# A hybrid RWKV-7 / FoX block on one core: product stages of several streams joined in bursts, FoX beside the RWKV chain, the lane inversion on GpSimd

## The chip, the core and the metric

The kernel runs on one core of a Trainium2 chip. A core has five engines with their own instruction queues: TensorE (matrix products and transposes, PE in the profile), VectorE (DVE), ScalarE (ACT), GpSimd (POOL) and SyncE (SP, which here only issues transfers). Each queue is worked off in its order, and an instruction may wait on semaphores of the others. The metric is the device time of one execution in microseconds.

## The reference, cut to what matters

One decoder block over 272 tokens (16 meta tokens and 256 of the input), width 2048. Two mixers run side by side, each with 16 heads of 64, and their outputs are gated and added; a SwiGLU feed-forward part follows.

```
proj = rms(h) @ w_in                          # RWKV, FoX and gate columns
y_a  = rwkv7(...)                             # below
y_b  = fox(...)                               # softmax attention with a forget gate
merged = sig(z_ga) * (y_a @ w_a) + sig(z_gb) * (y_b @ w_b)
h = h + merged @ w_o
h = h + (silu(gate) * up) @ w_down            # gate, up = rms(h) @ w_gu

def step(S, inp):                             # RWKV-7, a scan over the tokens, per head
    r_t, w_t, k_t, v_t, a_t, b_t = inp
    sa = einsum('bhvk,bhk->bhv', S, a_t)
    S  = S * w_t[:, :, None, :] + sa[..., None] * b_t[:, :, None, :] \
       + v_t[..., None] * k_t[:, :, None, :]
    return S, einsum('bhvk,bhk->bhv', S, r_t)
```

## The kernel before, in words

**Weight stream.** All weights come from memory in blocks of 128 x 1024 FP32 (`wload`). The SP queue loads a block into one of three `raw` tiles; ScalarE rounds it into `wh` (L322), VectorE forms the rest `wl = raw - wh` (L323), and TensorE multiplies both parts (L333 to L335, L392 and L394). Three tiles each of `raw`, `wh` and `wl` set how far the loads run ahead. A block of the projection holds 256 columns by 512 rows, so each of `k`, `v`, `r` and each gate needs four blocks.

**Order of the weight stream.** For each of four groups of four heads: `rwkv_jobs` (k, v, r, then the small decay and gate products), `fox_jobs` (q, k, v) and, after the first three groups, two gate tiles `zg` (four blocks each). The remaining gates follow group 3. `run` emits the load of a block ahead of the products of the block before it.

**Streams beside it.** Everything that isn't weight stream is written as generators ("streams"): `rwkv_bg` (the RWKV chain of a group), `fox_bg` (the attention of a group), `sums` and `norms` (FoX norms). A stream runs one stage up to its next `yield`, and the yielded number is the distance to its next stage in estimated ns of TensorE time. After every few weight products `slot` (L361) looks which streams are due and emits one stage of the one that has been due longest; `GAP` and `MIX` then keep the next one away. So the distances and `slot` fix at which place among the weight products a stage's products stand on TensorE, whose order is kept as it is written. On the other queues the framework places the instructions; what they hold is read from their order.

**RWKV chain.** In chunks of 64 tokens: `mat` products give the matrices NK; their strictly triangular 32 x 32 blocks go through memory (`d1`, L765 to L773) into `ln`, one matrix a lane, 112 lanes. Then the lane inversion (L831 to L838): 31 steps of two operations on `lx`, with growing rows, 62 dependent VectorE operations. The result goes from `lx` to memory (`d2`, `d3`, L841 and L843) and back into `X` (L847, L848), all issued on SP. After the distance `LANE` the stages `rhs`, `QT`, `X` follow, and then for each of four chunks `rhs`, `u` with `y`, `s` with `y`. The transposes `trbk`, `trv`, `tr0` prepare operands ahead of the inversion.

**FoX.** Per group and half (m = 0, 1): a bias on GpSimd (L1064 to L1070), scores `sc`, softmax, transposes `ppt` and `ptm`, and the product `po` with the values. The second half started after the first had ended.

PSUM has eight banks; four belong to the weight stream (`PSM`), four to the streams.

Of the kernel before, what the change touches and what calls it, by code (L numbers as in the profile page):

```python
# [62 lines left out]
LANE = 24000  # L63
GAP = 250
LERP = 2800
BIAS = 7000
STEP = 1000
NORM = 4200
SUMS = 2000
X_RS = 1400  # L70
X_SPREAD = 1400
X_V = 1900
X_SC = 1600
X_EXP = 1100
X_DIV = 2600
X_PT = 1400
Y_SQ = 1400
# [6 lines left out]
Y_BONUS = 1200  # L84
Y_TRBK = 1400
Y_TRV = 1100
Y_TR0 = 1600
Y_RHS = 1400
Y_U = 1400
Y_XT = 1400  # L90
Y_QT = 1200
Y_GN = 1400
# [5 lines left out]
def hybrid_block(ctx, tc, A, out, dbg=None):  # L98
# [18 lines left out]
    def aux_ps(name):  # L117
        return psa.tile([P, 512], F32, tag="aux", name=name)
# [224 lines left out]

    def spawn(gen, delay):
        streams.append([clock[0] + delay, gen])

    def stage(st):
        try:
            st[0] = clock[0] + (next(st[1]) or HOP)
        except StopIteration:  # L350
            streams.remove(st)

    def pe_mm(out_, lhsT, rhs, start, stop, skip=False):
# [316 lines left out]
    def rwkv_bg(g, box):  # L670
# [15 lines left out]
        nc.scalar.activation(sq, kk, AF.Square)  # L686
        yield Y_SQ
        kn_ = rw.tile([P, 12], F32, tag="kn", name=f"kn{g}", bufs=2)
# [4 lines left out]
        backs = [spread(kr_, m, L, f"kx{g}{m}") for m in range(2)]  # L693
        yield Y_SPREAD
        for m in range(2):
# [37 lines left out]
        split(*parts, sq[:, :, :T])  # L733
        yield Y_AB

# [3 lines left out]
        for m in range(2):  # L739
            pss = [aux_ps(f"mat{g}{m}{h}") for h in range(2)]  # L740
            for c in range(4):
                for h in range(2):
                    pe_mm(pss[h][:, c * P:(c + 1) * P], bk[hb(h), m, c].rearrange("p x t -> p (x t)"),
                                     ar[hb(h), :, m, tok(c)], start=True, stop=True)
            for h in range(2):
                nc.vector.tensor_tensor(NK[:, h, 4 * m:4 * m + 4, :], pss[h].rearrange("p (c w) -> p c w", w=P),
                                        bcast(mup, 4), op=ALU.mult)
            yield Y_MAT
        pss = [aux_ps(f"mat0{g}{h}") for h in range(2)]
# [28 lines left out]
        for h in range(2):  # L778
            for m in range(2):
                nc.gpsimd.tensor_copy(NK[0:HD, h, 4 * m:4 * m + 4, 0:HD],  # L780
                                      ar[hb(h), 0, m, NMETA:].rearrange("p (c t) -> p c t", t=HD))
        yield Y_NEXT

        bo = ot(f"bo{g}")
        for m in range(2):
# [5 lines left out]
            nc.gpsimd.tensor_scalar(bo[:, m, :], bo[:, m, :], vi("gn_b", m), None, op0=ALU.add)  # L791
        yield Y_BONUS

# [5 lines left out]
        for m in range(2):  # L799
            ps = aux_ps(f"trbk{g}{m}")  # L800
            for c in range(4):
                pe_tr(ps[:, c * P:(c + 1) * P], bkf[:, 4 * m + c, :], ident)
            nc.scalar.activation(BK[:, :, 4 * m:4 * m + 4, :].rearrange("p h c d -> p c h d"),
                                 ps.rearrange("p (c h d) -> p c h d", h=2, d=HD), AF.Copy)
            yield Y_TRBK
        ps = aux_ps(f"trv{g}")
# [7 lines left out]
        yield Y_TRV  # L814
        ps = aux_ps(f"tr0{g}")
# [15 lines left out]
        for s_ in range(31):  # L831
            n, w = s_ // 3 + 1, 31 - s_
            tv, xv = lt[:, 0:n, s_ + 1:], lx[:, 0:n, s_ + 1:]
            nc.vector.tensor_tensor(tv, lx[:, 0:n, s_:s_ + 1].to_broadcast([LANES, n, w]),
                                ln[:, s_:s_ + 1, s_ + 1:].to_broadcast([LANES, n, w]), op=ALU.mult)
            nc.vector.tensor_tensor(xv, xv, tv, op=ALU.add)
            if s_ % 4 == 3:
                yield STEP  # L838
# [10 lines left out]
        yield LANE  # L849

# [3 lines left out]
        def step(c, S, BK, SV, NK, X, Y):  # L854
# [24 lines left out]
            for h in range(2):  # L879
                nc.vector.tensor_copy(SV[0:nt, h, mine, :], pv2(ps)[h * HD:h * HD + nt])  # L880
            yield Y_U
            if not last:
# [20 lines left out]
            if not first:  # L903
                nc.scalar.activation(Y.rearrange("p (m c) v -> p m c v", m=2)[:, :, c, :], pv2(psy), AF.Copy)
            yield HOP

# [7 lines left out]
        next(meta_steps)  # L914
        yield Y_XT
        ps = aux_ps(f"QT{g}")
# [6 lines left out]
        next(meta_steps)  # L923
        yield Y_QT
        ps = aux_ps(f"X12{g}")
# [22 lines left out]
        nc.vector.tensor_tensor(Y, Y, s2.unsqueeze(2).to_broadcast([P, 8, HD]), op=ALU.mult)  # L948
        yield NORM
        ps = aux_ps(f"yT{g}")  # L950
# [28 lines left out]
    def fox_jobs(g):  # L979
# [18 lines left out]
        def norms():  # L998
            while len(done) < 2:
                yield  # L1000
            yield from rsqrt_steps(fx, hr, hs, [P, 20], "ht")
            yield X_RS

            nc.vector.tensor_tensor(hs[:, 0:8], hs[:, 0:8], hr[:, 0:8], op=ALU.mult)
            backs = [spread(hr[:, 8:20], m, L, f"fx{g}{m}") for m in range(2)]
            yield X_SPREAD
            for m in range(2):
                nc.vector.tensor_tensor(kn[:, m, :], kn[:, m, :], backs[m](), op=ALU.mult)
            yield
            ready.append(1)  # L1010

        def post(dst, n):
            def f(pss):
# [14 lines left out]
                if dst is vv:  # L1028
                    spawn(fox_bg(g, qn, kn, vv, hs, hr, ready), HOP)
                else:  # L1030
                    spawn(sums(sqs, dst, n), SUMS)
                    if dst is kn:
                        spawn(norms(), PREP)
# [5 lines left out]
    def fox_bg(g, qn, kn, vv, hs, hr, ready):  # L1039
# [18 lines left out]
        cmb = cmask.unsqueeze(1).to_broadcast([P, 2, P])  # L1058
        for m in range(2):

# [13 lines left out]
            nq = [NMETA + P, L]  # L1074
            cq_ = [slice(0, nq[0]), slice(nq[0], nq[0] + nq[1])]
# [5 lines left out]
            for t in range(2):  # L1081
                n = nq[t]
                for h in range(2):
                    s = sc_t[h, t]
                    nm = fx.tile([P, 1], F32, tag="nm", name=f"nm{g}{m}{h}{t}", bufs=4)
                    bb = b1[:, h, :] if t == 0 else bias[:, h, :]
                    nc.vector.tensor_tensor_reduce(s[:, :n], pss[h][:, cq_[t]], bb, 1.0, -3.0e38, op0=ALU.add,
                                                   op1=ALU.max, accum_out=nm)
                    r = hr[:, qc(t, m, h)]
                    nc.vector.tensor_scalar(nm, nm, -1.0, r, op0=ALU.mult, op1=ALU.mult)  # L1090
                    nc.scalar.activation(s[:, :n], s[:, :n], AF.Exp, scale=r, bias=nm,
                                         accum_out=sums[:, 2 * t + h:2 * t + h + 1])
            yield X_SC + X_EXP
# [5 lines left out]
            yield X_DIV  # L1099


            ptm = aux_ps(f"ptm{g}{m}")
            pts = []
            for h in range(2):
                ppt = aux_ps(f"ppt{g}{m}{h}")
                for c, t, k in ((T - 96, 0, 1), (0, 0, 0), (P, 1, 0), (T + 32, 1, 1)):
                    pe_tr(ppt[:, c:c + P], sc_t[h, t][:, k * P:(k + 1) * P], ident)
                pe_tr(ptm[:NMETA, h * P:(h + 1) * P], sc_t[h, 1][:, 2 * P:L], ident)
                pT = fx.tile([P, 416], F32, tag="pT", name=f"pT{g}{m}{h}", bufs=2)
                nc.scalar.activation(pT, ppt[:, :416], AF.Copy)  # L1110
                pts.append(pT)
            nc.scalar.activation(pM[:NMETA], ptm[:NMETA, :2 * P].rearrange("p (h q) -> p h q", h=2)[:, :, 96:], AF.Copy)
            yield X_PT
            po = aux_ps(f"po{g}{m}")
            for i in range(3):
                for h in range(2):
# [9 lines left out]
            yield  # L1126

# [263 lines left out]
```

## Time and profile before

| | |
|---|---|
| Median of three timed runs | 1566.58 us (1565.39 to 1569.84) |
| The profiled execution | 1564.75 us, of which the span of its instructions 1563.0 us |
| TensorE | 10,225 instructions |
| VectorE | 1,854 instructions, the inversion 248 of them |
| GpSimd | 194 instructions |
| Granted TensorE clock | 1.000 |
| Bytes moved | 283.33 MB, 181 GB/s on average |

The profile is of one execution. Busy time is the union of an engine's instructions; times in the timeline run from the span's start. The streams end at about 607 us, with the last transposes `yT`; what follows (the rest of the gates, branch products, output projection, feed-forward part) the change doesn't touch.

### The profile page before, as it was taken

The page shows a single profiled execution, that of the slowest core. Times are in us where ns is not written, and L with a number is a line of the kernel's source. Part 1 is how long each engine was busy: PE and PEld are TensorE (multiplying, and loading weights), DVE is VectorE, ACT ScalarE, POOL GpSimd, SP SyncE. Part 2 cuts the span into 40 slices and gives each one's busy share as a digit, 9 for nine tenths or more (in the row PEclk, how much of TensorE's full clock was granted, in tenths as well). Part 3 has the DMA queues.
Part 4 walks back from the last instruction along what each step waited for, and adds up shares of the span by engine and source line. Part 5 has one row for each costly group of instructions (what it writes and reads, how often), then busy time and mean ns, then how long its engine had stood idle before and what let it go on. Part 6 is the DMA issues. An engine that isn't in the chain of part 4 may idle for free.

```text
span 1563.0 us, 26173 instructions
## 1 busy us (share of the span) xinstructions
PE 1553.5 (99%) x10225; PEld 1366.3 (87%) x10225; DVE 1015.7 (65%) x1854; ACT 766.8 (49%) x1118; POOL 104.3 (7%) x194
## 2 busy tenths in 40 slices
PE   9999999999999999999999999999999999999998
PEld 9999988989889888999888888888888888888887
DVE  7878688677768856875655666566566656444443
ACT  6655455465445544654445554454445544333332
POOL 2121103102203100000000000000000000000000
PEclk9999999999999999999999999999999999999999
DMA  7556546546545566777666666666666666666664
GB/s 243 173 154 173 158 126 179 157 119 168 166 135 148 161 182 192 248 225 227 189 182 179 188 186 190 188 188 189 188 189 189 185 193 187 188 202 199 187 200 131
DMA packets 211483, 283.33 MB, mean 181 GB/s; under 512 B 23888, under 2 KB 128352, under 8 KB 211360
## 3 DMA queue, kind: packets, MB, share of 16 engines
q1 hardware_dynamic: 206752, 277.53, 60.8%
q10 hardware_dynamic: 4608, 4.13, 0.8%
q8 instruction: 80, 1.31, 0.4%
q14 instruction: 43, 0.35, 0.1%
HBM read 274.43 MB, written 7.19 MB: 180 GB/s over the span
## 4 chain that ended last, share of the span: by engine, by line
PE 94%; DVE 3%; DMA 1%; ACT 1%; issue 1%; SPq 0%; POOL 0%; DVEq 0%; ACTq 0%
PE up L392 10%; PE gt L392 10%; PE zg L392 7%; PE dn L1255 5%; PE dn L1253 5%; PE dn L1254 5%; PE up L394 5%; PE gt L394 5%; PE zg L394 3%; PE f L333 2%; PE f L392 2%; PE f L335 2%; PE f L334 2%; PE br L334 2%; PE br L335 2%; PE br L333 2%
## 5 line engine op out<-in xcount | busy, mean ns | idle before, releaser
L323 DVE TENSOR_TENSOR wl<-raw,wh 128x1024 fp32r<-128x1024 f32 (+1 forms) x496 | 605.3, 1221 | 439.7 <-ACT wh L322 437.8
L322 ACT ACTIVATE wh<-raw 128x1024 fp32r<-128x1024 f32 (+1 forms) x496 | 521.2, 1052 | 624.5 <-PE dn L1254 144.4
L392 PE MATMUL gt<-hts,wh 128*128 128x512 f32 x704 | 245.0, 394 | 0.0
L392 PE MATMUL up<-hts,wh 128*128 128x512 f32 x704 | 244.9, 394 | 0.0
L394 PE MATMUL gt<-hts,wl 128*128 128x256 f32 x660 | 186.2, 282 | 0.0
L394 PE MATMUL up<-hts,wl 128*128 128x256 f32 x660 | 186.0, 282 | 0.0
L392 PE MATMUL zg<-xhl,wh 128*128 128x512 f32 x512 | 184.3, 403 | 0.0
L392 PEld LDWEIGHTS up<-hts,wh 128*128 128x128 f32 x704 | 130.1, 188 | 26.4
L392 PEld LDWEIGHTS gt<-hts,wh 128*128 128x128 f32 x704 | 130.1, 188 | 26.3
L1254 PE MATMUL dn<-wh,acl 128*128 128x512 f32 x352 | 139.5, 396 | 0.0
L1253 PE MATMUL dn<-wh,ach 128*128 128x512 f32 x352 | 139.5, 396 | 0.0
L1255 PE MATMUL dn<-wl,ach 128*128 128x512 f32 x352 | 139.5, 396 | 0.0
L394 PE MATMUL zg<-xhl,wl 128*128 128x256 f32 x480 | 135.0, 281 | 0.0
L394 PEld LDWEIGHTS up<-hts,wl 128*128 128x128 f32 x660 | 124.7, 189 | 1.8
L394 PEld LDWEIGHTS gt<-hts,wl 128*128 128x128 f32 x660 | 124.7, 189 | 1.8
L392 PEld LDWEIGHTS zg<-xhl,wh 128*128 128x128 f32 x512 | 94.5, 188 | 20.8 <-issue 1.8
L394 PEld LDWEIGHTS zg<-xhl,wl 128*128 128x128 f32 x480 | 90.6, 189 | 1.1
L1255 PEld LDWEIGHTS dn<-wl,ach 128*128 128x128 f32 x352 | 66.3, 188 | 16.2
L1254 PEld LDWEIGHTS dn<-wh,acl 128*128 128x128 f32 x352 | 66.3, 188 | 16.2
L1253 PEld LDWEIGHTS dn<-wh,ach 128*128 128x128 f32 x352 | 66.3, 188 | 16.1
L333 PE MATMUL f<-xhl,wh 128*128 128x272 f32 x256 | 77.7, 303 | 0.0
L335 PE MATMUL f<-xhl,wl 128*128 128x272 f32 x256 | 73.8, 288 | 0.0
(459 smaller groups left out, 2777.6 us busy)
## 6 DMA issues: line engine op xcount, KB each, us to landing
raw<-in_w_gate_up_dram SPq DMA_DIRECT2D x176, 512.0 KB, 3.6
raw<-in_w_in_dram SPq DMA_DIRECT2D x160, 512.0 KB, 4.2
raw<-in_w_down_dram SPq DMA_DIRECT2D x88, 512.0 KB, 4.7
raw<-in_w_o_dram SPq DMA_DIRECT2D x32, 512.0 KB, 4.6
raw<-in_w_branch_a_dram SPq DMA_DIRECT2D x16, 512.0 KB, 3.9
raw<-in_w_branch_b_dram SPq DMA_DIRECT2D x16, 512.0 KB, 3.8
zgd<-zg ACTq DMA_DIRECT2D x30, 128.0 KB, 2.4
gate<-zgd SPq DMA_DIRECT2D x15, 256.0 KB, 5.8
```

Of the source, the lines that this page charges most:

```text
L322: nc.scalar.activation(wh[:prow, cs_], raw[:prow, cs_], AF.Copy)
L323: nc.vector.tensor_tensor(wl[:prow, cs_], raw[:prow, cs_], wh[:prow, cs_].bitcast(F32), op=ALU.subtract)
L333: nc.tensor.matmul(ps, wh, ah, start=first, stop=False)
L334: nc.tensor.matmul(ps, wh, al, start=False, stop=False)
L335: nc.tensor.matmul(ps, wl, ah, start=False, stop=last)
L392: nc.tensor.matmul(ps.rearrange("p (a t) -> p a t", a=2), wh, act, start=first, stop=last)
L394: nc.tensor.matmul(ps[:, :T], wl, act[:, 0, :], start=False, stop=False)
L1253: nc.tensor.matmul(box[t], ah[:, kt, ts_], wh[:, k, :], start=first, stop=False)
L1254: nc.tensor.matmul(box[t], al[:, kt, ts_], wh[:, k, :], start=False, stop=False)
L1255: nc.tensor.matmul(box[t], ah[:, kt, ts_], wl[:, k, :], start=False, stop=last)
```

## The change

It has four parts.

1. **Bursts.** A yield may now give a second number, the PSUM banks that the stage after it needs; a stage with such a number is a product stage. `slot` emits a due stage without products first and alone, as before. Otherwise it takes all due product stages, in the order in which they came due, as long as their banks together are at most four, and emits them one behind the other. If there is only one, it holds it back by up to `HOLD` = 2000 when another that would fit is due within that time.
2. **Distances.** Several are longer, among them `X_SPREAD`, `X_PT`, `Y_TRBK`, `Y_QT`; `BIAS` goes from 7000 to 28000. Three yields are dropped, so that the transposes of bk, and those of v with tr0, are one stage each.
3. **FoX.** The bias of the second half is emitted during the first half, its scores in the stage of the first half's `po`. The small transposes into the bank `ptm` go into a free part of `ppt`, with one copy for each head into pM in place of one for both.
4. **Inversion.** The 62 operations run on GpSimd in place of VectorE. Each waits for the one before it, as on VectorE.

```diff
-    def spawn(gen, delay):
-        streams.append([clock[0] + delay, gen])
+    def spawn(gen, delay, banks=0):
+        streams.append([clock[0] + delay, gen, banks])
...
-        due = [st for st in streams if st[0] <= clock[0]]
-        if due:
+        due = sorted((st for st in streams if st[0] <= clock[0]), key=lambda st: st[0])
+        group = [st for st in due if not st[2]][:1]
+        if due and not group:
+            banks = 0
+            for st in due:
+                if banks + st[2] <= 8 - PSM:
+                    group.append(st)
+                    banks += st[2]
+            if (len(group) == 1 and clock[0] < due[0][0] + HOLD and
+                    any(st[2] and st[0] > clock[0] and st[0] < due[0][0] + HOLD and banks + st[2] <= 8 - PSM
+                        for st in streams)):
+                return
+        if group:
             clock[2] = 0.0
-            stage(min(due, key=lambda st: st[0]))
+            for st in group:
+                stage(st)
             clock[1] = clock[0] + max(GAP, MIX * clock[2])
...
-            yield Y_RHS
+            yield Y_RHS, 2
...
             tv, xv = lt[:, 0:n, s_ + 1:], lx[:, 0:n, s_ + 1:]
-            nc.vector.tensor_tensor(tv, lx[:, 0:n, s_:s_ + 1].to_broadcast([LANES, n, w]),
-                                ln[:, s_:s_ + 1, s_ + 1:].to_broadcast([LANES, n, w]), op=ALU.mult)
-            nc.vector.tensor_tensor(xv, xv, tv, op=ALU.add)
+            nc.gpsimd.tensor_tensor(tv, lx[:, 0:n, s_:s_ + 1].to_broadcast([LANES, n, w]),
+                                    ln[:, s_:s_ + 1, s_ + 1:].to_broadcast([LANES, n, w]), op=ALU.mult)
+            nc.gpsimd.tensor_tensor(xv, xv, tv, op=ALU.add)
             if s_ % 4 == 3:
                 yield STEP
...
-        for m in range(2):
+        def biases(m):
...
-            yield BIAS
+            return b1, bias
...
+        bs = biases(0)
+        yield BIAS, 2
+        sums = scores(0, *bs)
+        for m in range(2):
             yield X_SC + X_EXP
...
+            if m == 0:
+                bs = biases(1)
+            yield X_DIV, 2
-            ptm = aux_ps(f"ptm{g}{m}")
             pts = []
             for h in range(2):
                 ppt = aux_ps(f"ppt{g}{m}{h}")
+                pe_tr(ppt[:NMETA, 3 * P:], sc_t[h, 1][:, 2 * P:L], ident)
...
-                pe_tr(ptm[:NMETA, h * P:(h + 1) * P], sc_t[h, 1][:, 2 * P:L], ident)
                 pT = fx.tile([P, 416], F32, tag="pT", name=f"pT{g}{m}{h}", bufs=2)
                 nc.scalar.activation(pT, ppt[:, :416], AF.Copy)
+                nc.scalar.activation(pM[:NMETA, h, :], ppt[:NMETA, 480:], AF.Copy)
                 pts.append(pT)
...
+            if m == 0:
+                sums = scores(1, *bs)
             nc.scalar.activation(yb[:, 2 * g + m, :], po[:, :T], AF.Copy)
```

What this does to the queues shows at two places. The first is the SP queue from the last transfers of group 0's matrices into `ln` to the transfers of its inverse into `X` (`raw` are weight blocks, `d` the blocks in memory). Before:

```order
L773 DMA ln_1477<-d_1474 4x1024 x4
L318 DMA raw<-in_w_in_dram 128x4x256 x7
L1064 DMA bias_2016<-ncd 128x544
L318 DMA raw<-in_w_in_dram 128x4x256 x4
L841 DMA d_1475<-lx_1666 352x1x32 x2
L841 DMA d_1475<-lx_1666 32x10x32
L843 DMA d_1476<-lx_1666 16x1x32 x4
L847 DMA X_1668<-d_1475 32x8x32 x3
```

In the changed kernel (a line number of before is 2 to 18 higher here):

```order
L791 DMA ln_1512<-d_1509 4x1024 x4
L320 DMA raw<-in_w_in_dram 128x4x256 x6
L858 DMA d_1510<-lx_1699 352x1x32 x2
L858 DMA d_1510<-lx_1699 32x10x32
L860 DMA d_1511<-lx_1699 16x1x32 x4
L864 DMA X_1701<-d_1510 32x8x32 x3
```

The transfers that wait for `lx` stand five weight blocks earlier, behind six blocks after `ln` in place of eleven. The first block behind them is the third block of group 1's `k`; before it was the fourth of its `v`. In the other groups they move by six, five and six blocks.

The second is TensorE at group 0's first chunk, among the products of the next group's `r`. Before, the stages u and y stand apart from everything else, and so does each FoX stage:

```order
L335 MATMUL r_1_2366<-xhl,wl 128x258
L355 MATMUL u_2425<-R_2406,X_1668 64x64 x4
L355 MATMUL y_2430<-S0-1_2342,ar_1275 64x64 x4
L333 MATMUL r_1_2366<-xhl,wh 128x258
```

In the changed kernel the transposes of the second half's probabilities follow in the same burst:

```order
L337 MATMUL r_1_2250<-xhl,wl 128x258
L360 MATMUL u_2463<-R_2410,X_1701 64x64 x4
L360 MATMUL y_2468<-S0-1_2325,ar_1284 64x64 x4
L364 MATMUL ppt_2475<-ident,s_165 16x128
L364 MATMUL ppt_2475<-ident,s_164 128x128 x2
L364 MATMUL ppt_2475<-ident,s_165 128x128 x2
L364 MATMUL ppt_2484<-ident,s_167 16x128
L364 MATMUL ppt_2484<-ident,s_166 128x128 x2
L364 MATMUL ppt_2484<-ident,s_167 128x128 x2
L335 MATMUL r_1_2250<-xhl,wh 128x258
```

FoX's second half now runs through the RWKV chain in such bursts. In the whole program the bursts between weight products go from 157 to 103, with the same number of products.

More of the change, by code (lines that the diff above doesn't have):

```diff
@@ L64 @@
 GAP = 250
+HOLD = 2000
 LERP = 2800
-BIAS = 7000
+BIAS = 28000
 STEP = 1000
@@ L70 @@
 X_RS = 1400
-X_SPREAD = 1400
+X_SPREAD = 2400
 X_V = 1900
@@ L75 @@
 X_DIV = 2600
-X_PT = 1400
+X_PT = 2200
+X_PT0 = 4400
 Y_SQ = 1400
@@ L84 @@
 Y_BONUS = 1200
-Y_TRBK = 1400
-Y_TRV = 1100
+Y_TRBK = 2600
 Y_TR0 = 1600
[L88 to L91, printed above, removed]
+Y_RHS = 1600
+Y_U = 1600
+Y_XT = 1600
+Y_QT = 2200
 Y_GN = 1400
@@ L342, in hybrid_block @@
     clock = [0.0, 0.0, 0.0]
-    def spawn(gen, delay):
-        streams.append([clock[0] + delay, gen])
+    def spawn(gen, delay, banks=0):
+        streams.append([clock[0] + delay, gen, banks])
     def stage(st):
         try:
-            st[0] = clock[0] + (next(st[1]) or HOP)
+            step = next(st[1]) or HOP
         except StopIteration:
             streams.remove(st)
+            return
+        step, st[2] = step if isinstance(step, tuple) else (step, 0)
+        st[0] = clock[0] + step
     def pe_mm(out_, lhsT, rhs, start, stop, skip=False):
@@ L686, in rwkv_bg @@
         nc.scalar.activation(sq, kk, AF.Square)
-        yield Y_SQ
+        yield Y_SQ, 1
         kn_ = rw.tile([P, 12], F32, tag="kn", name=f"kn{g}", bufs=2)
@@ L693, in rwkv_bg @@
         backs = [spread(kr_, m, L, f"kx{g}{m}") for m in range(2)]
-        yield Y_SPREAD
+        yield Y_SPREAD, 2
         for m in range(2):
@@ L733, in rwkv_bg @@
         split(*parts, sq[:, :, :T])
-        yield Y_AB
+        yield Y_AB, 2
         NK = nkt(f"NK{g}")
@@ L880, in step @@
                 nc.vector.tensor_copy(SV[0:nt, h, mine, :], pv2(ps)[h * HD:h * HD + nt])
-            yield Y_U
+            yield Y_U, 2
             if not last:
@@ L904, in step @@
                 nc.scalar.activation(Y.rearrange("p (m c) v -> p m c v", m=2)[:, :, c, :], pv2(psy), AF.Copy)
-            yield HOP
+            yield (HOP, 0) if last else (HOP, 1)
         S = [None]
@@ L914, in rwkv_bg @@
         next(meta_steps)
-        yield Y_XT
+        yield Y_XT, 2
         ps = aux_ps(f"QT{g}")
@@ L923, in rwkv_bg @@
         next(meta_steps)
-        yield Y_QT
+        yield Y_QT, 2
         ps = aux_ps(f"X12{g}")
@@ L1028, in f @@
                 if dst is vv:
-                    spawn(fox_bg(g, qn, kn, vv, hs, hr, ready), HOP)
+                    spawn(fox_bg(g, qn, kn, vv, hs, hr, ready), HOP, 2)
                 else:
-                    spawn(sums(sqs, dst, n), SUMS)
+                    spawn(sums(sqs, dst, n), SUMS, 1)
                     if dst is kn:
@@ L1092, in fox_bg @@
                                          accum_out=sums[:, 2 * t + h:2 * t + h + 1])
+            return sums
+        bs = biases(0)
+        yield BIAS, 2
+        sums = scores(0, *bs)
+        for m in range(2):
             yield X_SC + X_EXP
```

24 lines of the change are left out of this document (11 added, 13 removed).

## The prediction

> **What bounds the kernel now.** I read the page's table of busy time first, then the list of waits on TensorE, and then the timeline of single stretches.
>
> ```profile
> span 1563.0 us, 26173 instructions
> PE 1553.5 (99%) x10225; PEld 1366.3 (87%) x10225; DVE 1015.7 (65%) x1854; ACT 766.8 (49%) x1118; POOL 104.3 (7%) x194
> ...
> PE po L355 <- ACT pT L1110: 1.7, 1, 1.7
> PE warmup L296 <- DVE yb L293: 1.1, 1, 1.1
> ```
>
> TensorE has work for 99% of the span, and its longest wait in the whole run is 1.7 us. So the time is the length of TensorE's list of instructions, and an edit pays in two ways only: by a shorter list, or by a wait that the list did not have. All sums below stand against the profiled execution: 1564.75 us, of which 1563.0 are span and 1.75 lie around it. The median of the timed runs, 1566.58, is 0.1% above it. A difference of about 0.3% (4.7 us) is what a measurement of this kernel can tell from none.
>
> **What joining saves.** Three places of TensorE's timeline (start, duration, engine, line, result and operands): a lone stage of FP32 products, two such stages in one burst, and a stage of transposes, each among the weight-stream products of a projection.
>
> ```profile
> 178.21 0.28 PE L335 MATMUL r<-xhl,wl 128*128 128x258 f32 x1
> 178.42 0.45 PE L355 MATMUL rhs<-sv,NK 128*64 128x64 f32 x8
> 178.80 0.39 PE L333 MATMUL r<-xhl,wh 128*128 128x258 f32 x1
> 179.03 0.28 PE L334 MATMUL r<-xhl,wh 128*128 128x258 f32 x1
> ...
> 180.60 0.28 PE L335 MATMUL r<-xhl,wl 128*128 128x258 f32 x1
> 180.81 0.45 PE L355 MATMUL u<-R,X 64*64 64x64 f32 x8
> 181.09 0.40 PE L355 MATMUL y<-S0-1_2342,ar 64*64 64x64 f32 x8
> 181.42 0.39 PE L333 MATMUL r<-xhl,wh 128*128 128x258 f32 x1
> 181.64 0.28 PE L334 MATMUL r<-xhl,wh 128*128 128x258 f32 x1
> ...
> 113.64 0.29 PE L335 MATMUL f<-xhl,wl 128*128 128x272 f32 x1
> 113.77 0.60 PE L359 MATMUL trbk<-ident,bk 128*128 128x128 f32 x4
> 114.12 0.37 PE L333 MATMUL f<-xhl,wh 128*128 128x272 f32 x1
> 114.33 0.29 PE L334 MATMUL f<-xhl,wh 128*128 128x272 f32 x1
> ```
>
> Each r product starts 0.12 us after the one before when nothing lies between. From the last one before a burst to the second one behind it, two such steps, 0.24 us, are the stream's own. The lone stage takes 179.03 - 178.21 - 0.24 = 0.58 us for 8 products. Stages u and y together take 181.64 - 180.60 - 0.24 = 0.80 us for 16. Two lone ones would take 1.16, so a join of two such stages saves about 0.35 us: the entry and the exit. Four transposes take 114.33 - 113.64 - 0.25 = 0.44 us, 0.11 each, with no such fixed part; I price their joins at nothing.
>
> In the order of before, 100 stretches of FP32 products stand alone in the weight stream. In the changed order there are 75, of which some 70 border the stream and the rest border transposes. So 25 to 30 entries go: 25 x 0.35 = 9 us saved, 11 at most (30), and 7 if a change between FP32 products and transposes costs most of a fixed part too. The number of products is the same, 8,996 rows in both orders. Beside it the 1.7 us wait of stage po may go.
>
> **What the longer distances cost.** Weight products fill them, so nothing, as long as results are not wanted: the last stage, yT of head group 3, moves by 18 weight products and still has 124 of them ahead of the branch projections. The two narrower copies into pM (8 more on ACT, which is 49% busy) hide too. The freed VectorE time is worth nothing, since TensorE waits for VectorE nowhere for more than 1.1 us.
>
> **What the inversion on GpSimd costs.** The 62 operations of a group become one chain on GpSimd, and who waits for its end is the SP queue. In that queue's order, the seven transfers of lx into d2 and d3 wait for lx, and then six transfers into X follow. Behind them stand the weight loads. Before, at head group 0:
>
> ```profile
> 121.52 0.27 PE L359 MATMUL tr<-ident,v 128*16 128x128 f32 x1
> ...
> 121.74 0.31 POOL L716 MEMSET bk<- 128x256 f32 x1 [4.46 <-PE tr L359]
> ...
> 139.60 12.23 SPq L318 DMA_DIRECT2D raw<-in_w_in_dram  x4
> 153.37 1.98 SPq L841 DMA_DIRECT2D d<-lx  x3
> ...
> 161.06 1.52 SPq L318 DMA_DIRECT2D raw<-in_w_in_dram  x3
> ...
> 153.16 0.18 DVE L836 TENSOR_TENSOR lx<-lx,lt 112x11 f32<-112x11 f32 x1
> ...
> 165.19 1.06 ACT L322 ACTIVATE wh<-raw 128x1024 fp32r<-128x1024 f32 x1 [3.20 <-DMA raw<-in_w_in_dram]
> ...
> 166.28 1.23 DVE L323 TENSOR_TENSOR wl<-raw,wh 128x1024 fp32r<-128x1024 f32 x1 [3.00 <-ACT wh L322]
> ```
>
> The last operation on lx ends at 153.34, SP issues the first transfer 0.03 us later, and the next weight block is issued only at 161.06, three at once, since their buffers had been free. That block is split at 166.28 + 1.23 = 167.51. So a block queued behind the inversion is ready **14.2 us after the inversion's end**. Before this did no harm: eleven weight loads stood between ln and d, the held block was the fourth of v, and TensorE's list of waits has none on a split of it.
>
> The change leaves only six there. The held block in group 0 is the third of k, and between it and the tr transposes TensorE has 90 gate products and 48 products of k, with no burst among them:
>
> ```profile
> 120.49 0.39 PE L392 MATMUL zg<-xhl,wh 128*128 128x512 f32 x1
> ...
> 120.84 0.40 PE L392 MATMUL zg<-xhl,wh 128*128 128x512 f32 x1
> ...
> 144.12 0.29 PE L333 MATMUL k<-xhl,wh 128*128 128x272 f32 x1
> 144.25 0.29 PE L334 MATMUL k<-xhl,wh 128*128 128x272 f32 x1
> ```
>
> A pair of gate products takes 0.35 us and a k product 0.13: 45 x 0.35 + 48 x 0.13 = 22.0 us. In the other groups, counted the same way, it is 60 pairs, 24 k products and 1.1 us of transposes, 25.2; 50 pairs and 48 k products, 23.7; and 70 pairs with 0.7 us of transposes, 25.2. The chain starts about 0.5 us after the last tr transpose, since the reset of bk, which waits for tr, stands ahead of it on GpSimd (121.74 + 0.31 against 121.52). If the chain takes D, TensorE waits D + 14.2 + 0.5 less that time: D - 7.3, D - 10.5, D - 9.0 and D - 10.5. The sum over four groups is **4D - 37.3**.
>
> Now D. Nothing in the trace shows this operation on GpSimd; the nearest rows are these.
>
> ```profile
> L445 POOL TENSOR_TENSOR zd<-z x24: 612/640/1611, 52.3 to 445.7; 128x272 f32<-128x272 f32 x16, 128x256 f32<-128x256 f32 x8
> ...
> L1069 POOL TENSOR_TENSOR b<-b,cmask x8: 722/736/1702, 110.5 to 527.6; 128x256 f32<-128x256 f32 x8
> ...
> L138 POOL TENSOR_SCALAR_AFFINE_SELECT mup<-mup x4: 233/236/240, 2.3 to 2.9; 64x64 f32<-64x64 f32 x4
> ...
> L780 POOL COPY NK<-ar x16: 389/398/1464, 112.8 to 497.6; 64x256 f32<-64x256 f32 x16
> ...
> L834 DVE TENSOR_TENSOR lt<-lx,ln x124: 168/227/781, 123.8 to 535.3; 112x84 f32<-112x84 f32 x12, 112x30 f32<-112x30 f32 x8, 112x54 f32<-112x54 f32 x8, 112x72 f32<-112x72 f32 x8
> ```
>
> The 62 operations cover 3,982 elements a lane, 64 on average. From 612 ns at 256 elements and 640 at 272, a GpSimd operation with two inputs costs 1.75 ns an element, which puts 64 elements at 0.276 us: 62 x 0.276 = 17.1 us. From below, the 64-column selection (0.236, one input): 62 x 0.22 to 0.236, so 13.8 us at least. From above, the one with a broadcast input costs 0.12 us more at 256: 62 x 0.396 = 24.6 us. I take 17.1, the row with the same operation.
>
> To this comes waiting for VectorE. The copies into NK (389 ns at best) took up to 1464: the two engines hold each other up, and I count VectorE's weight split as time that GpSimd doesn't get.
>
> ```profile
> sum 64.00, DVE 22.27; mean DVE 5.57
> ```
>
> That is the split's busy time in four windows of 16 us behind tr: a share of 0.35. It lasts until the loads ahead of the held block are used up, some 15 us: 5.2 us. From below 0, from above 6.2 (all VectorE work but the inversion). So D = 17.1 + 5.2 = 22.3, with 13.8 and 30.8 as ends.
>
> The sum: 4 x 22.3 - 37.3 = 52 us of waits, less 9: 1564.75 + 43 = **1608 us**. The ends: 18 - 9 = +9, so 1574, and 86 - 7 = +79, so 1644.
>
> The Trainium skill gives another rate for GpSimd (GPSIMD Engine Reference, section 3.1): 4497 ns for a two-input add of 2,048 elements, 2.2 ns an element. Drawn through 612 ns at 256 this is an estimate of 0.19 us at 64 elements, D smaller by 5, and a time near 1587, inside the range.
>
> The same skill says (TensorE: Matmul & The Clock Gate, What's actually happening) that an idle window of about 3.4 us halves the clock until a busy window has passed. Four waits of this length would then cost an estimated 4 x 1.7 = 7 us more, 1615. No wait in this trace is that long and the granted clock is 1.00 throughout, so no run here shows it.
>
> **The rivals.**
> 1. *The chain is quick and only the joins count*: with D of 7.3 no block is late, with 9 the waits are 1.7 us in one group, and the time is 1564.75 - 9 = 1556 to 1558, or 2 less with the po wait gone. It needs 0.12 to 0.15 us an operation, below the GpSimd rows of 64 columns; for it speaks that no small two-input operation was measured. It decides at D = 11.6, where 4D - 37.3 equals 9: below that the kernel is not slower. Chance 0.11.
> 2. *Waits and joins cancel*: D of 11 to 13 gives 1562 to 1571. For it: an error of 2 us in each 14.2 or 22.0 would bring the lower end of my sum here. Chance 0.06.
> 3. *The two engines hold each other up far more*: the copy of 1464 ns lost 1.07 us at one meeting. If a dozen such meetings fall into a chain, D is 17.1 + 12 x 1.07 = 30, and VectorE splits its blocks late besides: over 1645. Against it: once the blocks ahead run out, VectorE has little to do and GpSimd runs free. Chance 0.07.
>
> **How the numbers follow.** My forecast, waits of 18 to 86 us in sum, has 0.76. Slower by over 0.3%: 0.76 + 0.07 = 0.83. Faster: 0.11. Same: 0.06. The range runs from 1564 to 1645: the forecast's two ends, 1574 and 1644, and below them most of rival 2 (0.04), which together hold 0.8.
>
> **What would show it.** In the changed profile TensorE should have four waits of some 12 to 15 us: in k of groups 1, 2 and 3, and in the gates behind group 3, released by the split of a block whose load SP issued 8 us after the last lx on GpSimd. The inversion's operations should average near 0.28 us and its chain span 22 us. A lone rhs should still take 0.58 us. I am wrong if the weight loads don't stop behind d, if the 62 operations take under 12 us, or if TensorE's waits stay near 2 us.

## The result and the profile after

The changed kernel takes **1660.17 us** (median of 4 runs, 1656.68 to 1661.5); the kernel before, run beside it, 1565.99 (1564.43 to 1569.84). The ratio is 1.059 (95% interval 1.057 to 1.062): slower by 94 us, above the upper end of the predicted range. The profiled execution took 1656.68 us.

From the page of the changed kernel: the span, the engines' busy time, two rows of the 40 slices, and the chain that ended last.

```profile
span 1654.9 us, 26173 instructions
...
PE 1559.7 (94%) x10225; PEld 1373.6 (83%) x10225; DVE 969.1 (59%) x1606; ACT 766.2 (46%) x1126; POOL 194.8 (12%) x442
...
PE   9995999499959959999999999999999999999999
...
PEclk9998999799979989999999999999999999999999
...
PE 83%; POOL 7%; DMA 3%; DVE 3%; issue 2%; ACT 1%; SPq 1%; ACTq 0%; POOLq 0%; DVEq 0%
```

TensorE has four slices with a hole, at 4 or 5 tenths, and the granted clock dips in the same places. GpSimd, with 12% of busy time, holds 7% of the chain that ends last. The list of what TensorE waits for (total, times, longest) says the same:

```profile
PE k L335 <- ACT wh L324: 59.3, 3, 21.3
PE zg L410 <- ACT wh L324: 18.6, 2, 17.4
PE mat L360 <- DVE bk L738: 3.9, 3, 3.4
```

In the timeline of the changed kernel the first of the four waits can be followed through the queues (start, duration, instruction, and in brackets the idle time before it and what ended it):

```profile
117.11 17.92 SPq L320 DMA_DIRECT2D raw<-in_w_in_dram  x6
154.74 1.99 SPq L858 DMA_DIRECT2D d<-lx  x3
...
162.48 12.90 SPq L320 DMA_DIRECT2D raw<-in_w_in_dram  x7
...
154.49 0.23 POOL L853 TENSOR_TENSOR lx<-lx,lt 112x11 f32<-112x11 f32 x1
...
166.30 1.06 ACT L324 ACTIVATE wh<-raw 128x1024 fp32r<-128x1024 f32 x1 [8.60 <-DMA raw<-in_w_in_dram]
...
167.41 0.60 PE L335 MATMUL k<-xhl,wh 128*128 128x272 f32 x1 [18.62 <-ACT wh L324]
...
320.70 0.60 PE L335 MATMUL k<-xhl,wh 128*128 128x272 f32 x1 [21.29 <-ACT wh L324]
...
471.86 0.60 PE L335 MATMUL k<-xhl,wh 128*128 128x272 f32 x1 [19.39 <-ACT wh L324]
...
619.24 0.79 PE L410 MATMUL zg<-xhl,wh 128*128 128x512 f32 x1 [17.44 <-ACT wh L324]
```

SP issues six weight loads, then its list comes to the transfers of `lx` and it stands from 135.03 to 154.74, until GpSimd's last operation on `lx` has ended at 154.72. Only behind the 13 transfers does the next weight load go out, at 162.48; it is split at 166.30, and TensorE goes on at 167.41 after 18.62 us. The places are those of the prediction: k of groups 1 to 3 and the gates behind group 3. The four waits are 76.7 us.

ScalarE's list stands in the same places: by the profile, the issue of a gate tile's transfer goes on only when a transfer of `lx` has landed (64.4 us in four waits, the longest 17.5). But it is free again 4.5 to 7.8 us before the held block has landed, so here the waits end with SP's load.

Outside group 1 the chain itself is hardly longer or shorter for the change. Its first operation on VectorE in group 0 before:

```profile
123.84 0.17 DVE L834 TENSOR_TENSOR lt<-lx,ln 112x31 f32<-112x31 f32 x1
```

The last one ended at 153.34. So 62 operations with 15.2 us of work, which stood among VectorE's weight splits, took 29.5 us from the first start to the last end (29.2, 30.8 and 31.8 in the other groups). On GpSimd they take 30.0 us (from 124.70 to 154.72), and 35.4, 29.9 and 30.7 in the other groups. What is new is the place of the transfers that wait for it, five or six weight blocks earlier in SP's list. No run keeps the chain on GpSimd with its transfers at the old place.

### The profile page after: what moved, and what is told of

The parts are those of the page before. It is cut to its first block, busy times and chain, and to the rows that moved or that the text cites. A ratio compares the mean times of both kernels' runs of the same rounds, so it can differ in the third digit from the quotient of the medians.

```text
span 1654.9 us, 26173 instructions
## 1 busy us (share of the span) xinstructions
PE 1559.7 (94%) x10225; PEld 1373.6 (83%) x10225; DVE 969.1 (59%) x1606; ACT 766.2 (46%) x1126; POOL 194.8 (12%) x442
## 4 chain that ended last, share of the span: by engine, by line
PE 83%; POOL 7%; DMA 3%; DVE 3%; issue 2%; ACT 1%; SPq 1%; ACTq 0%; POOLq 0%; DVEq 0%
PE up L410 10%; PE gt L410 10%; PE dn L1286 5%; PE dn L1285 5%; PE dn L1284 5%; PE up L412 5%; PE gt L412 5%; PE zg L410 4%; POOL lx L853 3%; POOL lt L851 3%; PE f L335 2%; PE f L410 2%; PE br L336 2%; PE br L335 2%; PE f L336 2%
## 5 line engine op out<-in xcount | busy, mean ns | idle before, releaser
L325 DVE TENSOR_TENSOR wl<-raw,wh 128x1024 fp32r<-128x1024 f32 (+1 forms) x496 | 605.4, 1222 | 490.1 <-ACT wh L324 488.6
L335 PE MATMUL k<-xhl,wh 128*128 128x272 f32 x128 | 39.7, 310 | 59.3 <-ACT wh L324 59.3
```

What stands on the lines that cost most here:

```text
L325: nc.vector.tensor_tensor(wl[:prow, cs_], raw[:prow, cs_], wh[:prow, cs_].bitcast(F32), op=ALU.subtract)
L335: nc.tensor.matmul(ps, wh, ah, start=first, stop=False)
```

## The experiments

| run | kernel | median us | ratio to before, 95% interval |
|---|---|---|---|
| e1_inv_dve | changed, inversion on VectorE | 1574.3 | 1.0065 (1.0053 to 1.0077) |
| e2_before_inv_pool | before, inversion on GpSimd | 1631.0 | 1.042 (1.041 to 1.044) |
| e3_pool_queue | changed, transfers issued by GpSimd | 1632.0 | 1.043 (1.041 to 1.044) |
| e4_inv_dve_no_join | e1 without joins | 1563.5 | 0.9991 (0.9982 to 0.9999) |
| e5_mat_alone | e1, first `mat` stage alone | 1564.1 | 0.9995 (0.9986 to 1.0003) |
| e6_half_chain | e3, 16 of 31 steps | 1600.5 | 1.022 (1.020 to 1.024) |
| e7_three_quarters | e3, 23 of 31 steps | 1617.0 | 1.034 (1.032 to 1.035) |
| e8_like_joins | e1, like stages joined only | 1563.0 | 0.9987 (0.9978 to 0.9996) |
| e9_idle_chain | e5 and an unread GpSimd chain | 1585.6 | 1.014 (1.011 to 1.017) |
| e10_no_reader | changed, nobody reads `lx` | 1583.1 | 1.011 (1.010 to 1.013) |
| e11_no_reader_mat_alone | e10, first `mat` stage alone | 1574.5 | 1.006 (1.005 to 1.007) |

### Which part brings the loss: e1 and e2

e1 puts the inversion of the changed kernel back:

```
-            nc.gpsimd.tensor_tensor(tv, lx[...], ln[...], op=ALU.mult)
-            nc.gpsimd.tensor_tensor(xv, xv, tv, op=ALU.add)
+            nc.vector.tensor_tensor(tv, lx[...], ln[...], op=ALU.mult)
+            nc.vector.tensor_tensor(xv, xv, tv, op=ALU.add)
```

> The changed kernel with the inversion back on VectorE; all else of the change stays. Theory (the weight loads wait on SP behind transfers that wait for the end of the GpSimd chain, and half clock follows each such wait): SP's list has the transfers of lx behind 12 weight loads after those of ln, not 6, so no wait over 4 us in k or zg, no stretch of half clock in the groups, 1555 to 1563 us: before less about 5 for the joins, plus at most 4 for small waits of the bursts. Rival (the joined bursts, the distances or FoX's new place bring the loss): 1640 or more. By my prediction's size of the joins (9 us): 1557.

e2 makes the opposite edit in the kernel before, and no other.

> The kernel before with only the inversion moved to GpSimd. Theory: the transfers of lx stand behind 7 weight loads after those of ln instead of 11 and a bias; four waits in k or the gates of 14 to 18 us each, some 2.9 us (one load's products) shorter than the changed kernel's 17.4 to 21.3, half clock for 3 to 4 us after each; 1625 to 1650 us. Rival (bursts, distances or FoX's place are needed for the loss): 1570 or less.

e1 measured 1574.3: the engine of the inversion carries 1660.2 - 1574.3 = 86 us. The four waits are gone, but 9.4 us against before are left, and the time is 11 us above the expected end of 1563: the rest of the change loses a little too (below). e2 measured 1631.0, inside what theory said, so the loss needs neither bursts nor distances. Its waits are shorter than expected, 11 to 13 us a group. From TensorE's list of waits in e2:

```profile
PE po L355 <- ACT pT L1110: 22.8, 2, 11.7
PE k L333 <- ACT wh L322: 11.8, 2, 6.6
PE zg L392 <- ACT wh L322: 10.2, 2, 5.4
```

Two of them show up on a product of FoX, which needs ScalarE's copy into `pT`. ScalarE's list in the timeline of e2:

```profile
156.58 0.33 ACTq L1155 DMA_DIRECT2D zgd<-zg  x1
156.96 0.52 ACT L1110 ACTIVATE pT<-ppt 128x416 f32<-128x416 f32 x1 [12.94 <-DMA d<-lx]
```

The copy stands behind the issue of a gate tile's transfer, and both go on only when a transfer of `lx` has landed: the end of GpSimd's chain is waited for in ScalarE's list as well.

Of the 66.7 us by which e2's span is longer than before's, such waits explain some 49. In and behind them TensorE works 33.2 us at a granted clock of 0.50; at full clock that work would take about half as long, so some 17 us are an estimate of what the clock costs. The two together are about the whole loss.

### What the joins are worth: e4, e5, e8

e4 takes the grouping out of `slot` and leaves the distances:

```
-        group = [st for st in due if not st[2]][:1]
-        if due and not group:
-...
+        group = due[:1]
```

> The first experiment's kernel with one stage a stretch (no joined bursts, no holding back); the distances, FoX's order and the inversion on VectorE stay. Theory (a join saves about 0.33 us only where neighbours have the same array form): 4 to 7 us slower than the first experiment. My prediction's size: 7 to 11 us slower. Rival (joins are worth nothing, or their bunched waits give it back): within 2 us of it.

It is not slower than e1 but 10.8 us faster, which none of the three expected. Set side by side by the number of weight products done, e1 is 3.3 us behind e4 in group 0, 11.0 at the 1500th product, and still 10.3 at the last product of the streams. Most of it comes in one burst, between groups 0 and 1. TensorE and VectorE there in the timeline of e1, and the granted clock in its windows (window, length, busy, clock, DMA share, GB/s):

```profile
227.92 0.45 PE L360 MATMUL u<-R,X 64*64 64x64 f32 x8
228.20 0.40 PE L360 MATMUL y<-S,ar 64*64 64x64 f32 x8
232.03 1.98 PE L360 MATMUL mat<-ar,bk 64*128 64x128 f32 x16 [3.44 <-DVE bk L738]
...
228.41 0.61 DVE L897 COPY sv<-u 64x128 f32<-64x128 f32 x2 [0.81 <-PE u L360]
228.94 0.71 DVE L729 SCALAR_TENSOR_TENSOR ar<-k,sig 128x544 f32<-128x544 f32 x1
...
231.81 0.18 DVE L739 TENSOR_TENSOR bk<-k,cs 128x32 f32<-128x32 f32 x1
```

```profile
226.00:232.00 6.00, 2.60 (x32) 1.00 0.50 153
232.00:235.60 3.60, 3.56 (x23) 0.53 0.00 0
235.60:240.00 4.40, 4.40 (x42) 1.00 0.36 96
```

The burst joins u, y and `mat`. The copy of u into `sv` can start only when the burst's own u products are done; behind it in VectorE's list stand six operations, `bk` the last, which `mat` needs: 228.94 to 231.99, 3.1 us on VectorE that run under weight products where the stages stand apart. TensorE waits 3.44 us for them and then works at about half clock for 3.6 us.

e5 takes only that stage out of the joins:

```
-        yield Y_AB, 2
+        yield Y_AB
```

> The first experiment's kernel (inversion on VectorE) with the stage that begins the products mat taken out of the joined bursts (in the first experiment it is joined to u and y between groups 0 and 1, its product waits 3.4 us for the tile bk, which VectorE makes behind its copy of u from the same burst, and TensorE then shows 0.72 of its clock for 6 us). Theory: the wait and the slow stretch go, 5 to 8 us faster than the first experiment, 1566 to 1570. Rival (the tile bk is late by itself, and the wait moves to the same product at its new place): within 2 us of the first experiment, 1572 to 1576.

1564.1, 10.2 us less than e1: more than the 5 to 8 expected. The order of the list before that place moves too, and with it go two waits of about 1 us each on weight splits in group 0 and the 3.3 us there. e5 has 96 stretches of other products between weight products where e4 has 137, and the same time, so the other joins are worth nothing that can be measured. From group 1 on, priced the way the prediction priced `rhs` and with the waits taken out, e1's 85 stretches cost 114.9 us and e4's 123 cost 118.0: about 0.1 us a join, not 0.35.

e8 joins only products of one form; the rest of the stages get no second number behind their `yield`:

```
-        yield Y_SQ, 1
+        yield Y_SQ
...
-            yield X_DIV, 2
+            yield X_DIV
```

> The first experiment's kernel with only stages of products of one form joined (rhs, u and y, s and y, po, sc); the stages of preparation, the transposes and the products pv run alone, as in the fourth experiment. Some 10 joins stay. Theory: 10 x 0.33 us less than the fourth experiment (1563.5), so 1559 to 1561. My prediction's size of a join gives the same here. Rival (every held-back stage makes a wait behind it): 1563 or more.

1563.0, the fastest kernel of the study, 0.13% under before; it is 0.5 us below e4 where 3 were expected, which the two runs can't tell apart. So 0.33 us a join is not borne out, and no loss by held-back stages either.

### Why the inversion on GpSimd costs so much: e3, e7, e6, e9, e10, e11

e3 lets GpSimd issue the transfers that wait for its own chain, so SP has no reason to stop:

```
-            nc.sync.dma_start(d2[...], lx[...])
+            nc.gpsimd.dma_start(d2[...], lx[...])
...
-                nc.sync.dma_start(X[...], d2v[h, q, :32])
+                nc.gpsimd.dma_start(X[...], d2v[h, q, :32])
```

> The changed kernel, inversion still on GpSimd, with the 13 transfers of lx and into X of each group issued by GpSimd instead of SP, so that no weight load stands behind them. Theory: the four waits of 17 to 21 us go; what may be left is the wait of VectorE for X at the transposition of X (3.4 us a group in the changed kernel, with the weight splits behind it), up to 8 us a group if the transfers land later from this queue; 1557 to 1590 us. Rival (GpSimd's work delays VectorE's and ScalarE's weight splits, whatever SP does): the waits stay, 1640 or more.

1632.0: a miss. 28 of the 86 us went, and four waits of 12 to 15 us were left. Behind the first queue stood a second one. VectorE's list of waits in e3 and its timeline, then what e7 and e6 leave of the same row:

```profile
DVE XT L930 <- DMA X<-d: 69.8, 4, 18.9
```

```profile
145.89 1.42 DVE L325 TENSOR_TENSOR wl<-raw,wh 128x1024 fp32r<-128x1024 f32 x1 [0.53 <-ACT wh L324]
163.93 0.45 DVE L930 STREAM_TRANSPOSE XT<-X 128x256 f32<-128x256 f32 x1 [16.62 <-DMA X<-d]
164.29 3.61 DVE L325 TENSOR_TENSOR wl<-raw,wh 128x1024 fp32r<-128x1024 f32 x3
```

VectorE comes to the transposition of X 16.62 us before X is there, and three weight splits that could run wait behind it. Before the change it came to it only at 161.16 and waited 0.07 us, so VectorE's list, too, asks for the result earlier. e7 shortens the chain in that kernel; e6 has `s_ % 2 == 0` in the same place:

```
+            if s_ % 4 != 1:
                 nc.gpsimd.tensor_tensor(tv, ...)
                 nc.gpsimd.tensor_tensor(xv, xv, tv, op=ALU.add)
```

> The third experiment's kernel with 8 of the 31 steps of the inversion left out (every fourth), so the inverse is not formed in full. Theory: the chain is 30 x 23/31 = 22 us, so each of the four waits is 7 to 8 us shorter, 5 to 7 us are left of 12 to 15, the half clock behind them stays; 1598 to 1606 us. Rival (loss goes with the amount of GpSimd's work): 58 x 23/31 = 43 us of loss, 1617.

> The third experiment's kernel (inversion and its transfers on GpSimd) with every second of the 31 steps of the inversion left out, so the inverse is not formed in full; the rest is unchanged. Theory (the four waits of 12 to 15 us are those of VectorE's transposition of X for the end of GpSimd's chain, with the weight splits behind it): a chain of about 15 us instead of 30 ends before the transposition is due, the four waits and the half clock behind them go, 1570 to 1580 us. Rival (GpSimd's work slows the splits by its mere amount): half of the loss of 58 us against the first experiment is left, about 1603.

Both times, 1617.0 and 1600.5, are the rival's. The traces say why mine were too low. From the list of VectorE's waits, e7 and then e6:

```profile
DVE XT L931 <- DMA X<-d: 51.1, 4, 14.4
```

```profile
DVE XT L931 <- DMA X<-d: 38.2, 4, 10.7
```

The waits on `X` go from 69.8 to 51.1 and 38.2 us, and the times by 15.0 and 31.5: about one for one. But the chain fell less than by its steps (in group 0 from 30.5 to 23.5 and 18.3 us), the transfers behind it still take 7.5 to 9.4 us, and in most groups VectorE came to the transposition earlier (in group 0 of e6 at 144.8, not 147.3). So the theory's mechanism stands and its sizes don't, and the times alone don't tell it from the rival. The next three runs do.

e9 gives GpSimd a chain that nobody waits for, beside VectorE's inversion in e5:

```
+            nc.gpsimd.tensor_tensor(gv, gx[...], ln[...], op=ALU.mult)
+            nc.gpsimd.tensor_tensor(gv, gv, lunit[...], op=ALU.add)
```

> The fifth experiment's kernel (inversion on VectorE, 1564.1) with a second chain of 62 operations on GpSimd beside it in each group, at the same place and of nearly the same shapes (7 rows of 11 at most), whose result nobody reads and no transfer waits for. Theory (the loss comes only from what waits for the end of GpSimd's chain): 1562 to 1568, no wait over 3 us on TensorE; VectorE's operations beside it may be held up by 1 us here and there as GpSimd's are. Rival (the loss goes with the amount of GpSimd's work beside VectorE, as the times of the sixth and seventh experiments alone would allow): about 58 us more, 1600 or above.

1585.6: neither. With two chains of short two-input operations side by side, VectorE's inversion itself slows; the groups of e5 and then of e9 (busy, mean ns):

```profile
L325 DVE TENSOR_TENSOR wl<-raw,wh 128x1024 fp32r<-128x1024 f32 (+1 forms) x496 | 605.3, 1221 | 448.4 <-ACT wh L324 442.6 <-PE v L337 4.7 <-DMA X<-d 0.6
L853 DVE TENSOR_TENSOR lx<-lx,lt 112x84 f32<-112x84 f32 (+23 forms) x124 | 27.9, 225 | 3.3
```

```profile
L325 DVE TENSOR_TENSOR wl<-raw,wh 128x1024 fp32r<-128x1024 f32 (+1 forms) x496 | 605.5, 1222 | 445.1 <-ACT wh L324 444.4
L855 DVE TENSOR_TENSOR lx<-lx,lt 112x84 f32<-112x84 f32 (+23 forms) x124 | 40.2, 325 | 3.3
```

So the engines do hold each other up. The weight splits, 605 us of VectorE's time, get no longer, but they come later: VectorE's chains take 32.7 to 34.1 us from first to last operation, in e5 28.1 to 29.6, TensorE's waits for splits rise from 1.0 to 13.9 us, and its clock is 0.50 for 10.2 us. e9 has VectorE run a chain that the changed kernel doesn't have there, so it couldn't settle the question for that kernel. e10 does: the changed kernel, GpSimd's chain in full, and transfers that read `ln`, its input.

```
-            nc.sync.dma_start(d2[...], lx[32 * j:32 * j + 32, :n])
+            nc.sync.dma_start(d2[...], ln[32 * j:32 * j + 32, :n])
```

> The changed kernel with the inversion on GpSimd in full (124 + 124 operations), but the transfers take the tile ln (which the chain reads) instead of its result lx, so the products use the uninverted matrix and nothing waits for the end of the chain. Theory: the four waits of 17 to 21 us and the half clock behind them go although GpSimd does the same work beside the same splits; what is left is the first experiment's loss by the joined stage mat: 1568 to 1577. Rival (the amount of GpSimd's work): 1630 to 1660.

> The same with the stage mat alone as in the fifth experiment. Against that one it tells what VectorE's freed 55 us are worth and what GpSimd's work costs the rest, with nobody waiting for the chain. Theory (both nothing, as predicted): 1561 to 1567, within 3 us of the fifth experiment (1564.1). Rival 1 (freed VectorE time pays): 1560 or less. Rival 2 (GpSimd beside the splits costs, as in the ninth experiment): 1570 or more.

e10 measured 1583.1, 77 us less than the changed kernel with every operation of the chain still there. The rival is out: the loss comes from waiting for the chain's end. e10 and e11 lie 6 and 7.5 us above the ranges expected, and 8.8 and 10.4 above e1 and e5; by its number alone e11 falls to its rival 2, work of GpSimd beside the splits. Its trace says otherwise for most of it. Product by product, e11 loses 7.0 us against e5 in one place of group 0 and 1.5 to 1.7 at the like place of the others; between them it gains 0.8 at most. The place in the timeline of e11:

```profile
123.50 1.99 SPq L858 DMA_DIRECT2D d<-ln  x3
...
137.58 8.16 SPq L320 DMA_DIRECT2D raw<-in_w_in_dram  x5
...
142.65 0.80 PE L410 MATMUL zg<-xhl,wh 128*128 128x512 f32 x1 [3.50 <-ACT wh L324]
```

With `ln` as their source the transfers stand behind 3 weight loads, not 12, and their own 14 us on SP hold the next load. That is SP's order once more, not GpSimd's work; the smaller losses of the other groups were not followed that far. And with no gain above 0.8 us anywhere, the 55 us that VectorE is freed of are worth next to nothing.

## Why the prediction was wrong

The direction, the mechanism and the places were right; the sum was 52 us short. Two of its terms failed: D, the length of a group's chain, came out too small (waits of 76.7 us in place of 52), and the joins had the wrong sign (some 9 to 11 us lost in place of 9 saved). A third, the half clock, was left out. Its terms, with what the runs showed:

| term | predicted us | measured us |
|---|---|---|
| four waits for the held weight block | 52 | 76.7 (the four rows above) |
| half clock behind them | 0 (an estimate of 7 stood beside the sum) | 9.0 (an estimate, from the four stretches below) |
| joins | -9 | +8.6 to +10.2 by the `mat` stage joined (e10 - e11, e1 - e5), +0.6 for the others (e5 - e4) |
| distances, FoX's place | 0 | -1.4 (e4 - before) |
| sum | +43 | +93.5 to +95.1, of 94.2 (1660.17 - 1565.99) |

The terms come from different runs, so a sum this close to the whole is in part luck.

**D, mis-sized.** The prediction made a chain of 17.1 us of operations and 5.2 of hold-ups, 22.3. Group 0 ran from 124.70 to 154.72, 30.0. GpSimd's groups in the changed kernel, and single operations of the chain:

```profile
L853 POOL TENSOR_TENSOR lx<-lx,lt 112x84 f32<-112x84 f32 (+23 forms) x124 | 52.0, 419 | 9.6
L851 POOL TENSOR_TENSOR lt<-lx,ln 112x84 f32<-112x84 f32 (+23 forms) x124 | 48.9, 394 | 9.4
```

```profile
125.02 0.25 POOL L853 TENSOR_TENSOR lx<-lx,lt 112x31 f32<-112x31 f32 x1
125.35 0.24 POOL L851 TENSOR_TENSOR lt<-lx,ln 112x30 f32<-112x30 f32 x1
...
130.48 1.17 POOL L851 TENSOR_TENSOR lt<-lx,ln 112x69 f32<-112x69 f32 x1
131.72 1.42 POOL L853 TENSOR_TENSOR lx<-lx,lt 112x69 f32<-112x69 f32 x1
...
149.20 0.30 POOL L851 TENSOR_TENSOR lt<-lx,ln 112x64 f32<-112x64 f32 x1
149.59 0.32 POOL L853 TENSOR_TENSOR lx<-lx,lt 112x64 f32<-112x64 f32 x1
```

A group's operations fill (52.0 + 48.9) / 4 = 25.2 us. In group 0 six of them, beside weight splits of VectorE, took 1.17 to 1.42 us where their like take 0.31 to 0.39, and lost 5.8 together, close to the 5.2 predicted. Without these the operations are 19.4. To them come 0.08 us between an operation's end and the start of the next, which needs its result (125.27 to 125.35), 4.8 in all, a term the prediction didn't have. So the base was 24.2, not 17.1: the line through rows of 256 and 272 elements gave 0.276 us at 64 elements, where the operations of 64 take 0.30 and 0.32 and the gap comes on top. In group 1 two operations on `bo` stand among the chain's, one of them 3.64 us late for VectorE's `bo`, and the chain takes 35.4. The prediction also never set D beside the 29.5 us that the chain took on VectorE.

**The range did not hold.** Three of the four chains lie inside the stated ends of D (13.8 to 30.8), group 1's does not. Put into the prediction's own sum, the four (126.0 in all, in place of 4D) give 126.0 - 37.3 = 88.7. From the chain's end to the held block's first product it is 12.6 to 12.8 us and not 14.2, 6.1 less in sum, and TensorE's work ahead of the held block (24.6, 27.3, 23.8 and 25.4 us for 22.0, 25.2, 23.7 and 25.2) and the chain's starts take off another 5.8: 76.7. With this and a saving of 9 the time would still be near 1632, inside the range, and 1641 with the half clock. What put it beyond 1645 was the joins. Rival 3 named a time over 1645 and nearly the right D, but for a wrong reason: a dozen meetings of 1.07 us, where group 0 had six of about 1 us; the rest of D was the slower base.

**Joins, the step that failed.** "A join saves about 0.35 us" came out in some bursts (s, y and po joined 1.60 us, apart 0.81 and 1.12) and not in others (u, y and po joined 1.75; `mat` with `fss`, sums of FoX's norms, 2.25 to 2.44, apart 1.28 and 1.16), and on average about 0.1 us is left. That it depends on the array form of neighbouring products was not tested by itself. And the prediction looked only at TensorE's list: it never asked what VectorE must do between two stages that now stand shoulder to shoulder.

**The clock.** The granted clock of the changed kernel behind the first wait, in windows (window, length, TensorE's busy time, clock, DMA share, GB/s), and then the four stretches of half clock in and behind the waits:

```profile
167.40:171.10 3.70, 3.25 (x13) 0.50 0.65 195
171.10:174.80 3.70, 3.70 (x31) 1.00 0.90 267
```

```profile
154.00:171.07 17.07, 3.22 (x12) 0.50 0.52 140
304.19:324.67 20.48, 3.53 (x14) 0.50 0.45 123
454.38:478.27 23.89, 5.97 (x24) 0.50 0.48 133
604.56:625.04 20.48, 5.33 (x15) 0.50 0.53 143
```

For 3.7 us after the wait the clock is 0.50 and k products start 0.225 us apart instead of 0.125; the 12 of them up to 171.09 lose 3.68 - 0.44 (a wait for `wl`) - 1.50 = 1.7 us, about half of the 3.22 us of work. In all four stretches TensorE works 18.05 us; half of that, 9.0, is an estimate of the loss, and the same products set beside those of e5, without the short waits for `wl`, give 9.3. The Trainium skill (TensorE: Matmul & The Clock Gate, What's actually happening) says that about 3.4 us of idleness halve the clock until a busy window of that length has passed. Here the trace agrees, after 18.62 us and after e1's 3.44 alike; the prediction cited the rule and left its 7 us out of the sum. In e9, though, the clock halved with no wait over 1.6 us ahead of it (last section), so a single wait of that length is not needed.

**What held.** Distances and FoX's place cost nothing (e4: 0.9991). A lone `rhs` still takes 0.57 to 0.58 us. Freed VectorE time is worth next to nothing (e11). The waits stand on the block whose load SP issued 7.8 us after the last `lx` (162.48 against 154.72).

## What to carry to other kernels

When a dependent chain moves to an idle engine, ask which in-order lists wait for its end (here SP's, and behind it VectorE's and ScalarE's), at which place in them the waiting instruction now stands, and what that nobody thinks of stands behind it. Here the chain took about 30 us on either engine in group 0; what differed was the place of its transfers in SP's list. When stages are joined, look at what another engine must do between them; a join that takes that work's cover away costs more than all entries saved. And price small operations from the start of one to the start of the next, on a chain that depends on itself.

## What the runs showed that was not expected

- Short two-input GpSimd operations (30 to 96 elements on 112 lanes) take 0.24 to 0.39 us, and a dependent one starts 0.07 to 0.08 us after the end of the one before.
- Seven operations of the chain of group 0 in e3 took about 0.9 us too long, each beside a weight split on VectorE, some of which took 1.37 to 1.42 us, not 1.22. The Trainium skill (GPSIMD Engine Reference, Specifications) names such contention with VectorE operations that have two inputs in SBUF; the traces agree. It is mutual between short operations (225 to 325 ns in e9) and hardly felt by long ones (1221 to 1222 ns on average).
- A TensorE wait of 3.4 to 3.5 us is as dear in clock as one of 18: 3.6 us at about half speed behind it in e1, against 3.7 to 6.4 behind the four long ones.
- The clock can halve without such a wait. In e9 it was 0.50 from 173.79 to 180.62; in the 3.42 us before, TensorE had been busy for 1.40 and no single wait was longer than 1.6.
